# Two PSUM banks of value sums and two of scores in the neighbourhood and windowed attention

## The chip, the cores and the metric

The kernel runs as one program on one core of a Trainium2 chip. The metric is the device time of one execution in microseconds (us). An execution is timed as a whole; the profile adds a span, from the first instruction to the last, and the time of the one execution that was profiled.

## The reference, cut to what matters

Two layers of an encoder over 1024 tokens of width 1024. Each layer projects the normed input once, and four groups of four heads read it: A (latent attention, dense), B (differential attention, dense), C (a window of 128 tokens on each side, with a sink) and D (a neighbourhood of 8 rows by 16 columns on the 64-wide grid, with a bias). The four outputs are joined, projected and added, then an MLP follows. Everything is float32.

```python
def swa_mixer(q, k, v, sinks, cos, sin):          # group C
    ...
    s = jnp.where(valid[None, :, None, None], s, NEG_INF)
    ...
    p = jax.nn.softmax(jnp.concatenate([s, sink], axis=-1), axis=-1)[..., :-1]
    o = jnp.einsum('bnkgqj,bnjkd->bnqkgd', p.astype(v.dtype), vb)

def na_mixer(q, k, v, rpb):                       # group D
    ...
        s = s + jnp.transpose(bias, (0, 2, 1, 3)).astype(jnp.float32)[None]
        p = jax.nn.softmax(s.reshape(B, NA_HEADS, GRID_W, kh * NA_COLS), axis=-1).reshape(s.shape)
        return jnp.einsum('bhwac,bawchd->bwhd', p.astype(v.dtype), v_r)

def reference(...):
    for l in range(DEPTH):
        ...
        mix = jnp.concatenate([rms_norm(y_a, out_g_mla[l]), y_b,
                               rms_norm(y_c, out_g_swa[l]), rms_norm(y_d, out_g_na[l])], axis=-1)
        x = x + mix @ w_out[l]
        h = rms_norm(x, norm2_g[l])
        x = x + jnp.square(jax.nn.relu(h @ w_up[l])) @ w_down[l]
```

## The kernel before

Products are made of two parts, high and low, in three passes (L219 to L221: high by high, high by low, low by high), the parts in the reduced format fp32r. Tokens are reordered for D so that its keys, like those of C, lie in a band: a block of 128 queries sees the key block of its own number and the two beside it.

In a layer the attention runs B, D, C, A, one after the other. `weave` steps through the generator of a group and, after a share of its steps, through a generator of other work, the fill: under B the latent projections and those of D, under D the projections of C and then the upward products of the latent group (`latp`), under C and A the part of the output projection that B's and D's outputs allow (`mix`). Between them it ticks the tails, which are the chains behind a finished head: denominators, their way through DRAM to be spread over the partitions, and norms. A framework orders the instructions of each engine from the dependences and a timeline of its own; on the chip every engine then works through its list in order, and waits on semaphores. SP issues nearly all DMAs, in order too.

The eight PSUM banks of this phase, each a tile of 128 by 512 float32, are split by name for the whole of it: two `mm` (projections and small things), two `tr` (transposes), three `sb` (scores) and one `pv` (value sums).

A head of D or C is `banded`. It has eight key blocks `kb` and makes the scores of query block `i` four blocks ahead: two matmuls into an `sb` bank (L987), an evacuation on VectorE with bias or mask and the running extreme (L1063 in D, L1094 in C), an exponential on ScalarE (L1066, L1097). For a key block, two or three 128x128 pieces are transposed into a `tr` bank (L996), ScalarE writes the high part (`pth`, L193), VectorE the low part (`ptl`, L187; three buffers of each), and `apply` adds the products with the values into `pv` (L1008 with the high part, L1009 with the low one). The 1024 queries fill two banks' worth of sums, so a head has two halves: half 0 takes key blocks 0 to 4, half 1 takes 3 to 7. `zeroed` opens a half with a product with zeros (L1037). `pv_out` takes a finished half out: ScalarE copies the lower 64 partitions (`pvt`, L757) and VectorE adds them to the upper 64 (`y` in D, `yc` in C, L187); `pvt` takes one of the three `ptl` buffers.

B and A are `dense`: scores of 128 queries by 1024 keys in two `sb` banks (L815, evacuated at L817, exponential L820), transposes (L851), value products (L839, L840). Other lines that appear: L266 and L275 are small products of the tails, L647 are transposes of a projection's output, L731 is a product of the latent group's shorter part.

Of the kernel before, what the change touches and what calls it, by code (L numbers as in the profile page):

```python
# [144 lines left out]
class Trunk:  # L145
    def __init__(self, ctx, tc, d, out):
        self.ctx, self.tc, self.nc, self.d, self.out = ctx, tc, tc.nc, d, out
        self.ahead, self.tails = 4, deque()
        pool = lambda **k: ctx.enter_context(tc.tile_pool(**k))
        self.const = pool(name="const", bufs=1)  # L150
        self.xp = pool(name="xp", bufs=8)
        self.big = pool(name="big", bufs=16)
        self.wp = pool(name="wp", bufs=3)
        self.cp = pool(name="cols", bufs=2)
        self.dram = pool(name="dram", bufs=1, space=bass.MemoryType.DRAM)
# [12 lines left out]
    @contextmanager  # L168
    def banks(self, **n):

        self.phase = getattr(self, "phase", 0) + 1
        with self.tc.tile_pool(name=f"ps{self.phase}", bufs=1, space=bass.MemoryType.PSUM,
                               reuse_waits="tile") as self.psum:
            self.nbanks = n
            yield

    def bank(self, tag, shape=(P, 512)):
        return self.psum.tile(list(shape), F, tag=tag, bufs=self.nbanks[tag], name=tag)

    def mm_ps(self):  # L180
        return self.bank("mm")
# [201 lines left out]
    def attention(self, l):  # L383
# [33 lines left out]
        def proj_c():  # L417
            tabs = self.table("64", rb, nc.gpsimd)
            for t in range(2):
                yield from one(T_CQ2[t], xs, self.ev_rope(tabs, qc[:, t]))  # L420
            yield from one(T_CK, xs, self.ev_rope(tabs, kc))
            yield from one(T_CV, xs, self.ev_plain(rb, self.to_values(vc)))
# [2 lines left out]
        y = {"b": [], "d": [], "c": [], "a": []}  # L425
        with ExitStack() as stack, ExitStack() as att:
            self.ap = att.enter_context(sbuf("att"))
            with self.banks(mm=2, tr=2, sb=3, pv=1):
                with sbuf("proj", "right") as self.pp:
                    first = [w_in(t) for t in self.WAVES[0]]  # L430
                    saved = d["x"]
# [32 lines left out]
                               fill, self.RB, self.LB, every=self.EV[0])  # L464
                    self.tails.append(self.mix_b(mix, y["b"], self.gsub[:, l:l + 1]))
                    fill = chain(proj_c(), self.latent_up(l, lat, rows, qa, ka, va))
                    self.weave(self.attn_d(l, qd, kd, vd, y["d"]), fill, self.RD, self.LD, every=self.EV[1])
                gout = lambda n: self.gout[n][:, l]
                self.tails.append(self.mix_group(mix, 2, y["d"], gout("na")))
# [24 lines left out]
                fill = groups_bd()  # L494
                self.weave(self.attn_c(l, qc, kc, vc, y["c"]), fill, self.RC, end=False, every=self.EV[2])
                self.tails.append(self.mix_group(mix, 4, y["c"], gout("swa")))
                self.weave(self.attn_a(l, qa, ka, krd, va, y["a"]), fill, self.RA, self.LA, every=self.EV[3])
                self.tails.append(self.mix_group(mix, 6, y["a"], gout("mla"), nc.vector))
            with self.banks(mm=8):
# [471 lines left out]
    def banded(self, qs, ks, v, y, j, finish, grid=False):  # L971
# [39 lines left out]
        for i in range(self.ahead):  # L1011
            score(i)
        yield True
        pv = self.zeroed()
        held = []
        for kb in range(8):
            if kb + self.ahead < 8:
                score(kb + self.ahead)
            part = parts(kb)
            if kb in (3, 4):  # L1020
                held.append(part)
            if kb <= 4:
                apply(pv, 0, kb, part)
            else:
                apply(pv, 1, kb, part)
            if kb == 4:
                self.pv_out(pv, y, j, 0, grid)
                pv = self.zeroed()
                for i, p in enumerate(held):
                    apply(pv, 1, 3 + i, p)  # L1030
            yield True
        self.pv_out(pv, y, j, 1, grid)

    def zeroed(self):

# [465 lines left out]
```

## Time and profile before

| | us |
|---|---|
| median of 3 runs | 2698.26 (2697.42 to 2702.37) |
| the profiled execution | 2701.14 |
| its span, first to last instruction | 2698.9 |
| busy in the span: TensorE (PE) | 2545.4 (94%) |
| VectorE (DVE) | 1944.6 (72%) |
| ScalarE (ACT) | 1438.1 (53%) |
| GpSimd (POOL) | 1151.6 (43%) |

The span leaves out 2.2 us of the execution's time. PE's share is of matmuls in flight: they are pipelined, and at half clock they count for longer, so 94% is not 94% of what the engine could do. The profile also gives the granted TensorE clock of a stretch, as a share of full speed: 1.00 is 2.4 GHz, 0.50 is 1.2 GHz, and its mean over the program is 0.969. In layer 0 the first score of D is at 323.47 us and the last value product of C at 511.52 us; in layer 1 they are at 1655.09 and 1845.38 us.

### The profile page before, as it was taken

To read this page: it belongs to the slowest core of one execution; us is meant where nothing else is said; L and a number is where in the kernel's file an instruction comes from. 1 tells how busy PE (TensorE), PEld (TensorE's weight loads), DVE (VectorE), ACT (ScalarE), POOL (GpSimd) and SP (SyncE) were. 2 spreads that over 40 slices of the span, in tenths; PEclk is the share of its full clock that TensorE was granted. 3 is DMA by queue.
4 is the path that set the end of the run, shared out by engine and by line. 5 is a ranking of instruction groups with operands and counts; after the bars stand their busy time and mean duration, and the time that the engine had idled before them with its cause. 6 is when DMAs were issued, how large, how long until landed. Compare 5 with 4: busy or idle time off the path is not lost.

```text
span 2698.9 us, 37585 instructions
## 1 busy us (share of the span) xinstructions
PE 2545.4 (94%) x12296; PEld 2109.5 (78%) x12296; DVE 1944.6 (72%) x3368; ACT 1438.1 (53%) x2591; POOL 1151.6 (43%) x816
## 2 busy tenths in 40 slices
PE   8999988999889999999999999789998999999997
PEld 6778876787778887888877788677886788778886
DVE  6777767784966669887568776577749666687776
ACT  4677756663534444444437776566635344444444
POOL 2555633301345554544425655332013455545552
PEclk9989998999999999999999899899999999999998
DMA  5534597421144457444245436963221444664431
GB/s 171 174 94 141 151 268 245 106 89 57 53 140 153 150 166 269 149 139 142 100 128 149 119 114 192 273 199 89 71 71 55 156 150 151 230 219 150 131 102 63
DMA packets 191666, 389.18 MB, mean 144 GB/s; under 512 B 23840, under 2 KB 33008, under 8 KB 191472
## 3 DMA queue, kind: packets, MB, share of 16 engines
q1 hardware_dynamic: 177648, 361.62, 43.3%
q10 hardware_dynamic: 13824, 25.17, 2.7%
q8 instruction: 97, 1.59, 0.2%
q14 instruction: 97, 0.79, 0.1%
HBM read 263.29 MB, written 123.41 MB: 143 GB/s over the span
## 4 chain that ended last, share of the span: by engine, by line
PE 73%; DVE 13%; DMA 5%; ACT 5%; issue 3%; POOL 1%; SPq 0%; DVEq 0%; ACTq 0%; POOLq 0%
PE u L219 8%; PE u L221 8%; PE u L220 8%; PE mm L219 6%; PE mm L220 5%; PE mm L221 5%; PE p L219 5%; PE p L220 5%; PE p L221 5%; PE sb L815 3%; DVE p L817 2%; DVE part L187 2%; PE tr L851 2%; ACT p L820 2%; DVE ptl L187 1%
## 5 line engine op out<-in xcount | busy, mean ns | idle before, releaser
L187 POOL TENSOR_TENSOR wl<-raw,wh 128x512 fp32r<-128x512 f32 x448 | 636.0, 1420 | 699.0 <-ACT wh L193 680.1
L193 ACT ACTIVATE wh<-raw 128x512 fp32r<-128x512 f32 x448 | 281.6, 629 | 575.0 <-PE u L220 314.6
L187 POOL TENSOR_TENSOR wl<-ws,wh 128x512 fp32r<-128x512 f32 (+1 forms) x120 | 151.2, 1262 | 431.2 <-ACT wh L193 427.1
L219 PE MATMUL u<-far,wh 128*128 128x512 f32 x768 | 301.5, 393 | 12.6 <-ACT ev L1247 8.3
L187 DVE TENSOR_TENSOR ptl<-tr,pth 128x512 fp32r<-128x512 f32 (+2 forms) x384 | 239.2, 629 | 88.4 <-ACT pth L193 87.2
L221 PE MATMUL u<-far,wl 128*128 128x512 f32 x768 | 300.8, 392 | 0.8 <-POOL wl L187 0.8
L187 DVE TENSOR_TENSOR raw<-raw 128x512 f32<-128x512 f32 x256 | 222.7, 875 | 107.9 <-POOL wl L187 54.2
L220 PE MATMUL u<-far,wh 128*128 128x512 f32 x768 | 300.5, 391 | 0.0
L193 ACT ACTIVATE pth<-tr 128x512 fp32r<-128x512 f32 (+2 forms) x384 | 206.2, 547 | 123.1 <-PE tr L851 67.2
L820 ACT ACTIVATE p<-p,nm 128x1024 f32<-128x1024 f32 x192 | 220.2, 1147 | 77.3 <-DVE nm L817 72.8
L219 PE MATMUL p<-far,wh 128*128 128x512 f32 x640 | 252.3, 394 | 7.5 <-DVE ev L187 7.5
L221 PE MATMUL p<-far,wl 128*128 128x512 f32 x640 | 251.0, 392 | 1.5 <-POOL wl L187 1.5
L220 PE MATMUL p<-far,wh 128*128 128x512 f32 x640 | 251.2, 392 | 0.0
L815 PE MATMUL sb<-stack 96*128 96x512 f32 x640 | 217.6, 422 | 13.1 <-DVE nm L817 12.8
L187 DVE TENSOR_TENSOR far<-act,far 128x512 fp32r<-128x512 f32 x224 | 210.4, 969 | 14.6 <-ACT far L193 14.6
L187 POOL TENSOR_TENSOR p<-p 128x1024 f32<-128x1024 f32 x64 | 153.5, 2402 | 110.8 <-ACT p L903 103.0
L219 PEld LDWEIGHTS u<-far,wh 128*128 128x128 f32 x768 | 145.4, 189 | 45.2 <-ACT ev L1247 9.2
L851 PE MATMUL tr<-ident,p 128*128 128x128 f32 x1024 | 163.2, 278 | 8.8 <-DVE ptl L187 6.0
L221 PEld LDWEIGHTS u<-far,wl 128*128 128x128 f32 x768 | 145.1, 189 | 32.2 <-POOL wl L187 1.6
L219 PE MATMUL mm<-xh,wh 128*128 128x512 f32 x416 | 168.3, 405 | 1.4 <-DVE part L187 1.2
L220 PEld LDWEIGHTS u<-far,wh 128*128 128x128 f32 x768 | 145.3, 189 | 30.1
L220 PE MATMUL mm<-xl,wh 128*128 128x512 f32 x416 | 165.3, 397 | 0.0
(248 smaller groups left out, 6110.1 us busy)
## 6 DMA issues: line engine op xcount, KB each, us to landing
act<-acts SPq DMA_DIRECT2D x224, 256.0 KB
raw<-in_w_up SPq DMA_DIRECT2D x128, 256.0 KB
acts<-ev SPq DMA_DIRECT2D x128, 256.0 KB
raw<-in_w_down SPq DMA_DIRECT2D x128, 256.0 KB
acts<-ev ACTq DMA_DIRECT2D x96, 256.0 KB
ws<-in_w_in SPq DMA_DIRECT2D x76, 256.0 KB
rz<-drows SPq DMA_DIRECT2D x40, 256.0 KB
stack<-kd SPq DMA_DIRECT2D x32, 256.0 KB
```

The costliest lines, as they stand in the source:

```text
L187: (eng or self.nc.vector).tensor_tensor(out=out, in0=a, in1=b, op=op)
L193: nc.scalar.activation(hi, src, AF.Copy)
L219: mm(ps, w[0], x[0][:, sl], start=start, stop=False)
L220: mm(ps, w[0], x[1][:, sl], start=False, stop=False)
L221: mm(ps, w[1], x[0][:, sl], start=False, stop=stop)
L815: self.nc.tensor.matmul(ps, q[:, qt * P:(qt + 1) * P], k[:, sl], start=i == 0, stop=i == len(passes) - 1)
L817: self.nc.vector.tensor_tensor_reduce(out=p[:, sl], in0=ps, in1=self.zero[:, 0:1].bitcast(F).broadcast_to([P, 512]), scale=-scale, scalar= ...
L820: self.nc.scalar.activation(p, p, AF.Exp, bias=nm[:, 1:2], scale=-1.0, accum_out=z)
L851: nc.tensor.transpose(t[:, k * 256 + i * P:k * 256 + (i + 1) * P], p[:, (j * 2 + k) * P:(j * 2 + k + 1) * P], self.ident)
```

## The change

For D and C the four banks of scores and value sums become two and two. The pool of these banks is closed and opened anew between B and D, and again between C and A, where it is three and one as before. In `banded` each half has its own `pv` bank: half 1 is opened when key block 3 comes, key blocks 3 and 4 are added to both halves at once, and half 0 is taken out after block 4 while half 1 goes on. The list `held` is gone.

```diff
-            with self.banks(mm=2, tr=2, sb=3, pv=1):
+            with self.banks(mm=2, tr=2), ExitStack() as own:
+                def tiles(**n):
+                    own.close()
+                    own.enter_context(self.banks(**n))
+
+                tiles(sb=3, pv=1)
...
                     fill = chain(proj_c(), self.latent_up(l, lat, rows, qa, ka, va))
+                    tiles(sb=2, pv=2)
                     self.weave(self.attn_d(l, qd, kd, vd, y["d"]), fill, self.RD, self.LD, every=self.EV[1])
...
                 self.tails.append(self.mix_group(mix, 4, y["c"], gout("swa")))
+                tiles(sb=3, pv=1)
                 self.weave(self.attn_a(l, qa, ka, krd, va, y["a"]), fill, self.RA, self.LA, every=self.EV[3])
...
-        pv = self.zeroed()
-        held = []
+        pv = [None, None]
         for kb in range(8):
             if kb + self.ahead < 8:
                 score(kb + self.ahead)
             part = parts(kb)
-            if kb in (3, 4):
-                held.append(part)
-            if kb <= 4:
-                apply(pv, 0, kb, part)
-            else:
-                apply(pv, 1, kb, part)
+            for half in range(2):
+                if 3 * half <= kb <= 4 + 3 * half:
+                    if kb == 3 * half:
+                        pv[half] = self.zeroed()
+                    apply(pv[half], half, kb, part)
             if kb == 4:
-                self.pv_out(pv, y, j, 0, grid)
-                pv = self.zeroed()
-                for i, p in enumerate(held):
-                    apply(pv, 1, 3 + i, p)
+                self.pv_out(pv[0], y, j, 0, grid)
             yield True
-        self.pv_out(pv, y, j, 1, grid)
+        self.pv_out(pv[1], y, j, 1, grid)
```

(The rest of the diff lets `bank` look up the pool and the count of a name.) Every engine has as many instructions of each kind as before; only their order and their waits change. In the rows below the changed kernel's lines are some higher: L996 there is the score product L987, L1005 the transposes L996, L1017 and L1018 the value products L1008 and L1009, L1041 the opening L1037, L824 A's score product L815, L221 to L223 the passes L219 to L221, L740 is L731, L277 is L275, L656 is L647, L860 is L851, L268 is L266.

TensorE, layer 0, the middle of D's first head. Before, half 1 is opened and the parts of blocks 3 and 4 are applied once more behind it:

```order
L1008 MATMUL pv<-pth,v 128x256
L731 MATMUL mm<-latp,wh 128x512 x2
L1009 MATMUL pv<-ptl,v 128x256
L996 MATMUL tr<-ident,p 128x128 x3
L266 MATMUL mm<-pairs,rz 128x2 x8
L996 MATMUL tr<-ident,p 128x128 x3
L1037 MATMUL pv<-zero 128x512
L1008 MATMUL pv<-pth,v 128x256
L1009 MATMUL pv<-ptl,v 128x256
L1008 MATMUL pv<-pth,v 128x384
L1009 MATMUL pv<-ptl,v 128x384
L996 MATMUL tr<-ident,p 128x128 x3
```

In the changed kernel, the same engine and layer at D's second head: the opening of a half (here half 0 of that head) and the value products.

```order
L1018 MATMUL pv<-ptl,v 128x384
L1017 MATMUL pv<-pth,v 128x384
L1005 MATMUL tr<-ident,p 128x128 x2
L1041 MATMUL pv<-zero 128x512
L1018 MATMUL pv<-ptl,v 128x384
L996 MATMUL sb<-stack 128x384 x4
L1005 MATMUL tr<-ident,p 128x128 x2
```

The opening stands between the products of the half before it and waits for no evacuation of that half; no products are repeated behind it.

TensorE, layer 0, where D begins. Before, D's scores stand among B's transposes and value products (L851, L839, L840) and the projections (`xh`, `xl`):

```order
L840 MATMUL pv<-ptl,v 128x256
L839 MATMUL pv<-pth,v 128x256
L840 MATMUL pv<-ptl,v 128x256
L987 MATMUL sb<-stack 128x384 x2
L851 MATMUL tr<-ident,p 128x128 x6
L987 MATMUL sb<-stack 128x384 x4
L851 MATMUL tr<-ident,p 128x128 x2
L275 MATMUL mm<-ident,rz 8x128
```

In the changed kernel D's first scores stand behind all of B, at the end of C's last projection, close ahead of the first latent product:

```order
L221 MATMUL mm<-xh_189,wh 128x512
L996 MATMUL sb<-stack 128x256 x2
L996 MATMUL sb<-stack 128x384 x2
L1041 MATMUL pv<-zero 128x512 x2
L222 MATMUL mm<-xl_190,wh 128x512
L223 MATMUL mm<-xh_189,wl 128x512
L221 MATMUL mm<-xh_193,wh 128x512
L222 MATMUL mm<-xl_194,wh 128x512
L223 MATMUL mm<-xh_193,wl 128x512
L996 MATMUL sb<-stack 128x384 x4
L1005 MATMUL tr<-ident,p 128x128 x4
L656 MATMUL mm<-ident,part 128x128 x4
```

The overlap of D's first scores with B is gone from the order, and the projections have moved forward into B's end.

TensorE, layer 0, where C ends. Before, A's scores (L815) stand among the last two heads of C:

```order
L1008 MATMUL pv<-pth,v 128x384
L275 MATMUL mm<-ident,rz 8x128
L987 MATMUL sb<-stack 128x256 x2
L815 MATMUL sb<-stack 128x512 x3
L996 MATMUL tr<-ident,p 128x128 x2
L1009 MATMUL pv<-ptl,v 128x384
L996 MATMUL tr<-ident,p 128x128
L1008 MATMUL pv<-pth,v 128x256
```

In the changed kernel they stand in one block behind C's last value product:

```order
L1005 MATMUL tr<-ident,p 128x128 x2
L1018 MATMUL pv<-ptl,v 128x384
L1017 MATMUL pv<-pth,v 128x384
L1018 MATMUL pv<-ptl,v 128x384
L1017 MATMUL pv<-pth,v 128x256
L1018 MATMUL pv<-ptl,v 128x256
L824 MATMUL sb<-stack 128x512 x18
L860 MATMUL tr<-ident,p 128x128 x2
```

All 42 of A's score products that stood ahead of C's end before stand behind it now, in each layer. From the opening of D's first half to C's last value product, TensorE's list of layer 0 goes from 98 score products of D and C, 168 transposes and 144 products of the fill, with those 42 of A and 4 of A's transposes, to 124, 176 and 125 with none of A's (128 score products counted from D's first score).

## Rows read from the trace of the kernel before

**Rows 1.** The page: busy time by engine, and the granted clock in 40 slices.
```profile
PE 2545.4 (94%) x12296; PEld 2109.5 (78%) x12296; DVE 1944.6 (72%) x3368; ACT 1438.1 (53%) x2591; POOL 1151.6 (43%) x816
...
PEclk9989998999999999999999899899999999999998
```

**Rows 2.** Stretches: busy PE, PEld, DVE, ACT, POOL; granted clock, DMA share, GB/s.
```profile
323.47:357.08 33.61, 33.22 (x188) 28.66 (x186) 20.29 (x52) 20.55 (x48) 17.00 (x13) 1.00 0.87 231
357.08:511.52 154.44, 132.13 (x699) 110.28 (x698) 108.70 (x271) 96.30 (x239) 51.01 (x43) 0.90 0.74 219
511.52:538.52 27.00, 26.17 (x168) 23.13 (x167) 19.78 (x44) 16.66 (x32) 9.66 (x10) 1.00 0.44 118
1686.60:1845.38 158.78, 133.65 (x701) 112.00 (x700) 109.62 (x272) 96.33 (x240) 47.60 (x43) 0.89 0.71 211
```

**Rows 3.** PE's waits, layer 0 (320 to 500 us): total, times, longest.
```profile
PE pv L1008 <- ACT pth L193: 5.6, 5, 2.4
PE pv L1037 <- DVE y L187: 4.6, 2, 3.0
PE mm L220 <- DMA latp<-lat: 3.2, 1, 3.2
PE pv L1037 <- DVE yc L187: 3.0, 1, 3.0
...
PE sb L987 <- DVE nb L1094: 1.2, 4, 0.4
```

**Rows 4.** PE's waits, layer 1 (1690 to 1860 us).
```profile
PE pv L1037 <- DVE y L187: 2.3, 4, 1.4
...
PE pv L1037 <- DVE yc L187: 0.7, 2, 0.3
PE sb L987 <- DVE nb L1063: 0.5, 1, 0.5
```

**Rows 5.** Timeline around two openings, layer 0: start, us, instruction, idle before, releaser.
```profile
414.44 0.80 PE L1037 MATMUL pv<-zero 128*128 128x512 f32 x1 [3.00 <-DVE y L187]
...
413.70 0.68 DVE L187 TENSOR_TENSOR y<-pv,pvt 64x512 f32<-64x512 f32 x1 [2.68 <-DMA yb<-y]
414.42 0.56 DVE L187 TENSOR_TENSOR ptl<-tr,pth 128x384 fp32r<-128x384 f32 x1
...
415.44 0.49 ACT L193 ACTIVATE pth<-tr 128x384 fp32r<-128x384 f32 x1 [3.72 <-PE pv L1008]
...
449.35 1.06 ACT L366 ACTIVATE sq<-y 128x1024 f32<-128x1024 f32 x1 [2.84 <-POOL y L187]
...
449.51 0.20 DVE L768 RECIPROCAL rz<-z 128x8 f32<-128x8 f32 x1 [2.85 <-POOL z L187]
...
450.32 0.80 PE L1037 MATMUL pv<-zero 128*128 128x512 f32 x1 [2.98 <-DVE yc L187]
```

**Rows 6.** Stretches of layer 0 at half clock; two follow the openings of rows 5.
```profile
398.27:401.68 3.41, 3.41 (x11) 3.10 (x12) 3.31 (x12) 2.22 (x8) 0.76 (x1) 0.50 0.98 284
411.92:418.75 6.83, 4.17 (x14) 3.38 (x14) 2.33 (x6) 1.36 (x3) 0.00 (x0) 0.50 1.04 300
449.47:456.29 6.82, 5.57 (x19) 4.95 (x20) 4.47 (x11) 4.21 (x11) 0.69 (x2) 0.50 1.02 330
```

**Rows 7.** A PE gap of 0.92 us, and the ten microseconds behind it.
```profile
427.79 0.38 PE L1008 MATMUL pv<-pth,v 128*128 128x256 f32 x1 [0.92 <-ACT pth L193]
...
427.00:437.00 10.00, 9.21 (x53) 8.02 (x54) 9.73 (x27) 8.48 (x24) 4.38 (x5) 1.00 0.58 202
```

**Rows 8.** The wait for the first latent operand in layer 1.
```profile
1702.92 0.79 PE L220 MATMUL mm<-latp,wh 128*128 128x512 f32 x1 [4.70 <-DMA latp<-lat]
```

**Rows 9.** Chain that ended last: what products cost PE one behind the other.
```profile
480.44 0.70 PE sb L815 x3
...
333.94 0.35 PE sb L987 x2
...
355.68 0.33 PE tr L996 x3
```

More of the change, by code (lines that the diff above doesn't have):

```diff
@@ L147, in __init__ @@
         self.ctx, self.tc, self.nc, self.d, self.out = ctx, tc, tc.nc, d, out
+        self.psum = {}
         self.ahead, self.tails = 4, deque()
@@ L172, in banks @@
         with self.tc.tile_pool(name=f"ps{self.phase}", bufs=1, space=bass.MemoryType.PSUM,
-                               reuse_waits="tile") as self.psum:
-            self.nbanks = n
+                               reuse_waits="tile") as pool:
+            self.psum.update({tag: (pool, bufs) for tag, bufs in n.items()})
             yield
     def bank(self, tag, shape=(P, 512)):
-        return self.psum.tile(list(shape), F, tag=tag, bufs=self.nbanks[tag], name=tag)
+        pool, bufs = self.psum[tag]
+        return pool.tile(list(shape), F, tag=tag, bufs=bufs, name=tag)
     def mm_ps(self):
```

## Prediction

> **What bounds the kernel now.** I read the page first: PE is busy for 94% of the span, VectorE for 72%, ScalarE for 53% [rows 1]. The whole is thus TensorE's, and only what makes TensorE wait, or run at half clock, is to be had. The change touches D and C alone, so next I cut both layers into stretches: the last of B from D's first score to D's first opening, D and C from there to C's last value product, and the first 27 us of A [rows 2]. In the first and the last PE is busy for 33.22 of 33.61 and 26.17 of 27.00 us. In the middle it is busy for 132.13 of 154.44 us in layer 0 and 133.65 of 158.78 in layer 1, at a mean clock of 0.90 and 0.89. So the middle stretches lose 22 and 25 us to waiting, and 0.10 x 154.44 and 0.11 x 158.78, 15 and 17 us, to the clock. No other engine is full there: VectorE has 108.70 of 154.44 us, ScalarE 96.30, the DMA engines a share of 0.74. The stretch runs in lock-step, each engine waiting in turn for the one before.
>
> The list of waits says where PE stands. At the opening of a `pv` bank it waits for VectorE's `y` or `yc`, the end of `pv_out`: 4.6 and 3.0 us in layer 0, 2.3 and 0.7 in layer 1, 10.6 us in all [rows 3, 4]. The other waits are for `pth`, for a latent operand from DRAM and for scores. Two openings make most of it, 3.00 and 2.98 us. The timeline shows what was late there [rows 5]: at the first VectorE stood for 2.68 us until the store of `yb` had left the buffer that `y` writes, at the second for 2.85 us in a reciprocal that waits for GpSimd, and ScalarE for 2.84 in a square that waits for GpSimd. Behind each of the two the clock is at 0.50 for 6.83 us [rows 6]; a gap of 0.92 us has no such stretch behind it [rows 7].
>
> **The change part by part.** No instruction is added or dropped. Four things move.
>
> *The opening no longer waits.* With a bank of its own, half 1 opens at key block 3, when its bank has long been taken out by the head before. All 10.6 us go if nothing else holds PE. But where VectorE or ScalarE is itself stuck behind a DMA or GpSimd, they stay stuck: PE may fill the second `tr` bank and apply what lies ready (a group of three transposes is 0.33 us, a value product as wide as a score product 0.175 [rows 9]), and then waits for `ptl`, which stands in VectorE's list behind the same `y`. I leave 1.0 us at each of the two long ones, and take -8.6; bounds -4.6 (both stay whole) and -10.6.
>
> *The clock.* At half rate 6.83 us do the work of 3.4, so the stretches of rows 6 cost 1.7, 3.4 and 3.4 us. A rest of 1.0 us at an opening is near the gap of rows 7, behind which the clock stayed. I take the first and one of the two long ones, -5.1; bounds 0 and -8.5.
>
> *D begins behind B.* The scores of D's first head no longer stand in B's end; the projections have taken their place, so PE has work there. What comes sooner is the first latent product. Between the middle of C's last projection (its reads release the tiles into which the operand is loaded) and that product PE now has 8 transposes and 7 value products less and two openings more: by rows 9, with the openings at the 0.233 of a product of 512 columns, 8 x 0.11 + 7 x 0.175 - 2 x 0.233 = 1.6 us. It already waits 3.2 and 4.7 us there [rows 3, 8], so it waits 1.6 longer in each layer: +3.2; bounds 0 (fewer of D's loads stand ahead of it in the queue of SP) and +3.2.
>
> *A begins behind C, and scores have two banks.* At C's end nothing stands between the last transposes and the last value products, which need 0.49 us of ScalarE and 0.56 of VectorE [rows 5]: +1.0 in each layer, +2.0, bounds 0 and +4. With two `sb` banks a score waits for the evacuation two before it, not three. Those waits are 1.2 and 0.5 us now [rows 3, 4]; I let them double, +1.7; bounds 0 and +6, which is the two stuck places of rows 5 felt once more at a score.
>
> The sum is -8.6 - 5.1 + 3.2 + 2.0 + 1.7 = -6.8 us. Against the profiled execution's 2701.14 that is 2694.3; against the median of the runs, which lies 2.9 lower, 2698.26 - 6.8 = 2691.5, a fall of 0.25%. About 0.2%, 5.4 us, is what a measurement of this kernel can tell from no change, so this is just beyond it.
>
> A second account checks that moving work between stretches is by itself neutral. From the order, layer 0's middle loses 42 score products of A and 19 of the fill at 0.233 us and 4 transposes of B's kind, and gains 30 of D's scores at 0.175 and 8 transposes at 0.11 [rows 9]: -14.2 - 0.4 + 5.3 + 0.9 = -8.4 us. B's end changes by 4.4 - 5.3 - 0.9 = -1.8, and A's beginning by +9.8 + 0.4 = +10.2. The three add up to nothing. So the middle has to shrink from 154.44 to 146.0 us for no change at all, and by my terms it comes to about 139 (layer 0 has 5.6 of the 8.6 us, all of the 5.1, and half of the costs).
>
> **The rivals.** *Nothing to measure.* The stuck engines hold PE all the same: the openings give only the 4.6 us that were not long stalls, the clock nothing, and 6.9 us of costs stand against it: +2.3, 2700.6; with the latent wait at its lower bound -0.9, 2697. For it: both long stalls have their cause outside the sums [rows 5]. Against it: ScalarE stood for 3.72 us for want of value products that waited behind the opening, which shows the lock-step at work.
> The Trainium skill, TensorE: Matmul & The Clock Gate, section HAM oscillation — how this bites in real kernels, tells of a kernel in which double-buffering PSUM gave no further gain; by that result the first two terms would be nothing and the sum +6.9, 2705. The trace's 10.6 us at the openings speaks against taking it over whole.
>
> *Slower: D and C lose their cover.* Before, 42 score products of A stand within C; after, they stand behind it. If the middle is set by the chain of VectorE and ScalarE, with its 108.70 us of VectorE in 154.44, and not by PE's share of work, it stays at 154.4 us, and PE's 8.4 us come on top in each layer: +16.8, 2715; with half of that, +8.4, 2707. It decides at 146.0 us for layer 0's middle: above that the layer is slower. For it: VectorE keeps nearly all its work in the middle while PE gives 8.4 us away. Against it: VectorE is busy for only 0.70 of the middle, and in the ten microseconds of rows 7 it did 9.73 of 10.00.
> The Trainium skill, Perfetto Trace Analysis, section Optimization Strategy, says that where the most contended engine changes over time, interleaving the regimes may help. The change does the reverse at both ends of D and C, and by that rule alone this rival would hold, at its +16.8. The trace agrees that the ends with overlap are the fuller ones (33.22 of 33.61 us).
>
> *That the change does nothing it says* the order excludes: the second opening stands at key block 3, with no product repeated behind it.
>
> **How the numbers follow.** I give the forecast, faster, 0.42; no measurable change 0.34; slower 0.24. The time is the forecast's, 2691.5. Its own range is 2676 to 2696: at the low end every term is at its better bound (-10.6 - 8.5 and no costs, -19, 2679) with a little for waits on `pth` (5.6 us in layer 0) that may go as well. The whole range reaches into the slower rival to some of its full price: 2676 to 2711.
>
> **What would show it.** Right: no waits at the opening (L1041 after) for `y` or `yc`; layer 0's middle, from the first opening to the last value product, well under 146 us; no half-clock stretch of 6.8 us behind the places where the third head of D and the first of C turn to half 1; the wait for the latent operand at about 4.8 and 6.3 us; waits of scores below 4 us in all. Wrong: waits for `ptl` or `pth` that grow by what the openings lose (then the first rival), or a middle above 146 us with PE waiting for scores or value products, and VectorE no busier (then the second). If the gain is much above 10 us, the lock-step cost more than PE's waits at the openings show.

## The result, and the profile after

The changed kernel takes 2719.59 us, median of 4 runs (2713.05 to 2725.22), against 2700.32 for the kernel before on the same chip (2697.42 to 2705.94): ratio 1.0064, 95% interval 1.0039 to 1.0089. In a second set (e4) it is 2717.88 us, ratio 1.0058 (1.0042 to 1.0075). It is 16 to 19 us slower; forecast was a gain of 6.8, in a range up to 2711. The profiled execution took 2713.05 us, its span is 2711.3.

The page of the changed kernel answers to [rows 1]: busy time by engine, and the granted clock in 40 slices.

```profile
PE 2559.2 (94%) x12296; PEld 2114.6 (78%) x12296; DVE 1942.2 (72%) x3368; ACT 1438.2 (53%) x2591; POOL 1148.6 (42%) x816
...
PEclk9989989999999999999999899899999999999998
```

The same number of instructions, and a TensorE that is busy 13.8 us longer, while the other engines are not. The page says no more, so next come the stretches, columns as in [rows 2]. In each layer they are D and C from the first opening to the last value product, from there to A's first value product, and on to A's 120th; in layer 0 also the rest of A.

```profile
358.40:503.10 144.70, 125.88 (x663) 103.69 (x661) 104.67 (x271) 95.36 (x251) 45.31 (x42) 0.91 0.80 236
503.10:521.20 18.10, 16.65 (x69) 13.22 (x70) 10.38 (x26) 8.58 (x16) 4.32 (x6) 0.81 0.09 30
521.20:582.60 61.40, 58.71 (x361) 50.79 (x359) 49.48 (x106) 40.84 (x72) 8.83 (x7) 0.97 0.34 93
582.60:636.60 54.00, 50.18 (x331) 42.64 (x329) 41.42 (x90) 36.22 (x62) 0.00 (x0) 1.00 0.16 55
...
1697.80:1841.60 143.80, 124.16 (x663) 101.27 (x661) 105.05 (x271) 95.62 (x252) 45.70 (x42) 0.92 0.81 238
1841.60:1860.50 18.90, 16.56 (x61) 13.39 (x62) 9.45 (x22) 8.06 (x14) 3.69 (x5) 0.73 0.10 29
```

And the kernel before, from C's last value product to A's first, in both layers:

```profile
511.50:514.20 2.70, 1.88 (x13) 1.44 (x11) 1.43 (x5) 2.62 (x6) 0.00 (x0) 1.00 0.40 114
...
1845.40:1848.10 2.70, 1.88 (x14) 1.46 (x12) 1.44 (x3) 2.63 (x6) 0.01 (x1) 1.00 0.47 138
```

The middle did shrink, from 154.44 and 158.78 us to 144.70 and 143.80. But 2.70 us between C and A have become 18.10 and 18.90, at a clock of 0.81 and 0.73. Before, A was 42 score products deep by C's end; now it starts from nothing, and its first value product comes 15.4 and 16.2 us later. By the prediction's count of moved work (its second account, for layer 0) that should have been 10.2.

TensorE's waits in D and C: first layer 0, to be held against [rows 3] (the opening is L1041 now, the score L996, the value product L1017).

```profile
PE sb L996 <- DVE nb L1067: 3.6, 3, 3.1
PE pv L1017 <- ACT pth L195: 3.4, 2, 2.0
...
PE mm L222 <- DMA latp<-lat: 1.8, 1, 1.8
PE sb L996 <- DVE nb L1098: 1.5, 1, 1.5
...
PE pv L1041 <- DVE yc L189: 0.9, 2, 0.7
PE mm L221 <- DMA latp<-lat: 0.8, 1, 0.8
```

And layer 1, against [rows 4, 8]:

```profile
PE pv L1017 <- ACT pth L195: 5.8, 5, 2.3
...
PE sb L996 <- DVE nb L1098: 2.3, 4, 1.1
PE mm L222 <- DMA latp<-lat: 2.1, 1, 2.1
PE sb L996 <- DVE nb L1067: 1.6, 2, 0.9
...
PE mm L221 <- DMA latp<-lat: 1.0, 1, 1.0
...
PE pv L1041 <- DVE y L189: 0.3, 1, 0.3
PE mm L740 <- DMA latp<-lat: 0.2, 1, 0.2
```

The openings wait 0.9 and 0.3 us, 1.2 in place of 10.6. Scores wait 3.6 + 1.5 + 2.3 + 1.6 = 9.0 us in place of 1.7. The latent operand is waited for less, not more: 1.8 + 0.8 = 2.6 us in layer 0 and 2.1 + 1.0 + 0.2 = 3.3 in layer 1, in place of 3.2 and 4.7.

The start of A in layer 0, from the chain that ended last:

```profile
503.10 0.40 PE pv L1018
503.53 0.60 ACT pvt L766
504.15 0.70 DVE yc L189
...
504.92 2.39 POOL yc L189
507.33 1.06 ACT sq L368
508.39 1.14 ACT p L829 x2
509.57 0.44 PE tr L860 x2
510.01 3.09 PE mm L268 x16
```

C's last product, its copy out of the bank, GpSimd's part of `yc`, and then on ScalarE the squares of `yc` ahead of A's first two exponentials: only at 509.57 is there a block of A to transpose, 6.5 us after C's last product. The other 11.6 us up to A's first value product are TensorE's own list: sixteen small products of a tail (L268), more of A's scores and transposes, and products of the output projection. The timeline of TensorE there (`sb<-stack` are A's score products), and two stretches by the clock, one in each layer:

```profile
503.33 4.87 PE L824 MATMUL sb<-stack 96*128 96x512 f32 x18
509.57 0.44 PE L860 MATMUL tr<-ident,p 128*128 128x128 f32 x2 [1.38 <-ACT p L829]
...
521.16 0.28 PE L848 MATMUL pv<-pth,v 128*128 128x256 f32 x1
...
510.00:516.90 6.90, 6.90 (x26) 6.08 (x25) 3.12 (x10) 2.90 (x6) 0.81 (x4) 0.51 0.00 0
1848.00:1858.30 10.30, 10.07 (x36) 8.90 (x37) 4.17 (x13) 3.85 (x9) 0.00 (x0) 0.50 0.01 2
```

TensorE issues 18 score products in a row, stands for 1.38 us, and from 510.0 on runs at half clock, 1.2 GHz, for 6.9 us; in layer 1 a stretch of 10.3 us begins in the same place. The kernel before has no half clock there: its first 27 us of A ran at 1.00 [rows 2].

### The profile page after: what moved, and what is told of

The parts are those of the page before. It is cut to its first block, busy times and chain, and to the rows that moved or that the text cites. A ratio compares the mean times of both kernels' runs of the same rounds, so it can differ in the third digit from the quotient of the medians.

```text
span 2711.3 us, 37601 instructions
## 1 busy us (share of the span) xinstructions
PE 2559.2 (94%) x12296; PEld 2114.6 (78%) x12296; DVE 1942.2 (72%) x3368; ACT 1438.2 (53%) x2591; POOL 1148.6 (42%) x816
## 4 chain that ended last, share of the span: by engine, by line
PE 71%; DVE 13%; DMA 6%; ACT 5%; issue 4%; POOL 1%; SPq 1%; DVEq 0%; ACTq 0%; POOLq 0%
PE u L221 8%; PE u L223 8%; PE u L222 8%; PE mm L221 6%; PE mm L222 5%; PE mm L223 5%; PE p L221 5%; PE p L222 5%; PE p L223 5%; PE sb L824 3%; DVE p L826 2%; PE tr L860 2%; DVE part L189 2%; ACT p L829 2%; DVE ptl L189 2%
## 5 line engine op out<-in xcount | busy, mean ns | idle before, releaser
L221 PE MATMUL u<-far,wh 128*128 128x512 f32 x768 | 301.7, 393 | 9.2 <-ACT ev L1251 5.9
L223 PE MATMUL u<-far,wl 128*128 128x512 f32 x768 | 300.9, 392 | 2.6 <-POOL wl L189 2.6
L221 PE MATMUL p<-far,wh 128*128 128x512 f32 x640 | 251.3, 393 | 8.1 <-DVE ev L189 8.1
L223 PE MATMUL p<-far,wl 128*128 128x512 f32 x640 | 250.8, 392 | 1.2 <-POOL wl L189 1.2
L824 PE MATMUL sb<-stack 96*128 96x512 f32 x640 | 221.9, 430 | 12.9 <-DVE nm L826 12.4
L221 PEld LDWEIGHTS u<-far,wh 128*128 128x128 f32 x768 | 145.3, 189 | 41.9 <-ACT ev L1251 7.2
L860 PE MATMUL tr<-ident,p 128*128 128x128 f32 x1024 | 166.0, 281 | 11.7 <-DVE ptl L189 7.5
L223 PEld LDWEIGHTS u<-far,wl 128*128 128x128 f32 x768 | 145.3, 189 | 34.0 <-POOL wl L189 3.5
L221 PE MATMUL mm<-xh,wh 128*128 128x512 f32 x416 | 168.2, 404 | 3.3 <-DVE part L189 3.2
L222 PEld LDWEIGHTS u<-far,wh 128*128 128x128 f32 x768 | 145.4, 189 | 30.6 <-DVE far L189 0.5
L826 DVE CUSTOM_DVE_ANT_0 p<-sb,zero,nm 128x512 f32<-128x512 f32 x192 | 142.6, 744 | 35.3 <-PE sb L824 30.6
```

What stands on the lines that cost most here:

```text
L221: mm(ps, w[0], x[0][:, sl], start=start, stop=False)
L222: mm(ps, w[0], x[1][:, sl], start=False, stop=False)
L223: mm(ps, w[1], x[0][:, sl], start=False, stop=stop)
L824: self.nc.tensor.matmul(ps, q[:, qt * P:(qt + 1) * P], k[:, sl], start=i == 0, stop=i == len(passes) - 1)
L826: self.nc.vector.tensor_tensor_reduce(out=p[:, sl], in0=ps, in1=self.zero[:, 0:1].bitcast(F).broadcast_to([P, 512]), scale=-scale, scalar= ...
L860: nc.tensor.transpose(t[:, k * 256 + i * P:k * 256 + (i + 1) * P], p[:, (j * 2 + k) * P:(j * 2 + k + 1) * P], self.ident)
```

## The experiments

Three things come with the change: other banks in D and C, another order of products in D and C, and pools that are closed and opened again between B and D and between C and A. To have banks without re-opening, some kernels keep one pool with a bank "flex" that is lent by name:

```python
if tag in ("sb", "pv"):
    sets = {"sb": ("sb0", "sb1"), "pv": ("pv0",)}[tag] + (("flex",) if self.shared == tag else ())
    self.turn[tag] += 1
    slot, n = sets[self.turn[tag] % len(sets)], 1
```

Banks are given as scores/values. "Early" is the changed order of products (the second group of sums opens at key block 3), "held" the older one. Medians are of 4 to 12 runs, ratios against the kernel before in the same set (2699.05 to 2702.84 us).

| run | B | D, C | A | order | re-opened | us | ratio (95%) |
|---|---|---|---|---|---|---|---|
| before | 3/1 | 3/1 | 3/1 | held | - | 2700 | 1 |
| after (e4) | 3/1 | 2/2 | 3/1 | early | B-D, C-A | 2717.88 | 1.0058 (1.0042, 1.0075) |
| e1 | 3/1 | 3/1 | 3/1 | held | B-D, C-A | 2735.01 | 1.0128 (1.0112, 1.0144) |
| e2 | 3/1 | 2/2 | 3/1 | early | - | 2710.07 | 1.0036 (1.0023, 1.0049) |
| e3 | 2/2 | 2/2 | 2/2 | early | - | 2713.15 | 1.0050 (1.0036, 1.0065) |
| e5 | 3/1 | 2/2 | 2/2 | early | B-D | 2692.18 | 0.9965 (0.9949, 0.9981) |
| e6 | 2/2 | 2/2 | 3/1 | early | C-A | 2738.15 | 1.0129 (1.0109, 1.0148) |
| e8 | 3/1 | 3/2, one `tr` | 3/1 | early | - | 2792.14 | 1.0326 (1.0305, 1.0347) |
| e9 | 3/1 | 2/1 | 3/1 | held | - | 2707.40 | 1.0018 (1.0004, 1.0031) |
| e10 | 3/1 | 2/2 | 2/2 | early | B-D, C-A | 2696.36 | 0.9986 (0.9977, 0.9996) |
| e11 | 3/1 | 2/2 | 2/2 | early | - | 2686.54 | 0.9960 (0.9948, 0.9973) |
| e12 | 3/1 | 2/2 | 2/2 | held | B-D | 2695.28 | 0.9990 (0.9980, 0.9999) |
| e13 | 2/2 | 2/2 | 2/2 | early | B-D | 2742.03 | 1.0164 (1.0144, 1.0183) |
| e14 | 3/1 | 3/1 | 2/2 | held | - | 2699.39 | 0.9999 (0.9989, 1.0010) |
| e15 | 3/1 | 2/2 | 2/1 | early | - | 2684.38 | 0.9945 (0.9931, 0.9960) |
| e16 | 3/1 | 2/2 | 2/1, then 3/1 | early | - | 2691.67 | 0.9970 (0.9959, 0.9982) |
| e17 | 3/1 | 2/2 | 2/2 | held | - | 2693.77 | 0.9983 (0.9973, 0.9993) |
| e18 | 3/1 | 2/2 | 2/1 | early | B-D, C-A | 2703.60 | 1.0007 (0.9994, 1.0020) |
| e19 | 3/1 | 3/1 | 3/1 | held | C-A | 2717.27 | 1.0064 (1.0050, 1.0077) |

Theory 1: the re-opening is the loss, since the order shows every instruction on the new banks behind the last one on the old. Theory 2: the third score bank of D and C is. The first four runs:

**e1_reopened**: the kernel before, its pool re-opened at both places.

```diff
+                    tiles(sb=3, pv=1)
                     self.weave(self.attn_d(...
+                tiles(sb=3, pv=1)
                 self.weave(self.attn_a(...
```

> The kernel before, with the pool of score and value banks closed and opened anew at both places, but with three and one banks throughout and the held parts as before. Theory 1 (the re-opening puts D behind B and A behind C, and that is the loss): about 2716 to 2722, as slow as the changed kernel or a little slower; from C's last value product to A's 120th value product about 79 us where the kernel before has 64.0 and 63.9, with a half-clock stretch in it; openings still wait for the evacuation, some 8 to 11 us. Theory 2 (two score banks are the loss, through 9 us of waits of scores where there were about 2): within 4 us of the kernel before, 2697 to 2704.

**e2_shared**: the new banks and order, lent by name, nothing re-opened.

```diff
-            with self.banks(mm=2, tr=2, sb=3, pv=1):
+            with self.banks(mm=2, tr=2, sb0=1, sb1=1, flex=1, pv0=1):
...
+                    self.shared = "pv"
                     self.weave(self.attn_d(...
...
+                self.shared = "sb"
                 self.weave(self.attn_a(...
```

> The changed banded with two and two banks in D and C, but no pool is closed: one bank of the pool is lent, as third score bank in B and A and as second value bank in D and C. Theory 1: D's scores overlap B again and A's overlap C, the openings do not wait, so faster than the kernel before by the gain of the middle beyond what moved, 1.3 and 6.1 us, and with the loss at the seams gone: 2688 to 2697. Theory 2: scores wait as in the changed kernel, 7 us more than before, and it stays at 2710 or more.

**e3_whole**: two and two for the whole phase, which also shares the first projections' banks out anew.

```diff
-            with self.banks(mm=2, tr=2, sb=3, pv=1):
+            with self.banks(mm=2, tr=2, sb=2, pv=2):
...
-                        return [(self.bank(a), self.bank(b)) for a, b in (("sb", "sb"), ("sb", "tr"), ("tr", "pv"))]
+                        return [(self.bank(a), self.bank(b)) for a, b in (("sb", "sb"), ("tr", "tr"), ("pv", "pv"))]
```

> Two score and two value banks for the whole phase of attention, B and A too, nothing re-opened. Theory 1: the seams overlap, so no loss there; B and A have one score bank less, each score tile of which needs two banks, so PE waits for VectorE more in B and A: the waits of L815 were 36.0 us with weight loads counted, and a tenth to a half more of these is 4 to 18 us; 2695 to 2712. Theory 2: slower than the changed kernel, above 2720, as scores lack a bank everywhere.

**e4_again**: the changed kernel once more, in the same set.

> The changed kernel once more, for a second profile. Both theories: 2713 to 2725; from C's last value product to A's 120th about 79.5 us in both layers, of which some 5 are the clock, and the middles near 144.7 and 143.9 us. If the half-clock stretch at A's beginning is absent in this profile and the time is the same, the clock there was chance and not the loss.

Re-opening alone costs 34 us, more than the whole change, so theory 1 holds; but without it the change still loses 0.36%, so it isn't all. The next four separate the two seams and the banks.

**e5_seam_bd**: the changed kernel without the second re-opening; A stays on two and two.

```diff
-                tiles(sb=3, pv=1)
                 self.weave(self.attn_a(...
```

> The changed kernel with one re-opening left: three score banks and one value bank are traded for two and two between B and D, and A then stays on two and two, so nothing is re-opened between C and A. Theory 1 (the seam at A's start is the costly one: the middle is at its break-even in the changed kernel, A's beginning some 5 us a layer over it): A loses its seam, 2706 to 2713 us, and A's gap before its first key loads (2.2 us in layer 1) is gone. Theory 2 (the seam between B and D is the costly one): no gain at A, and A pays for its third score bank, 2716 to 2724 us.

**e6_seam_ca**: the other seam alone, B on two and two.

```diff
-                tiles(sb=3, pv=1)
+                tiles(sb=2, pv=2)
                 with sbuf("proj", "right") as self.pp:
...
-                    tiles(sb=2, pv=2)
                     self.weave(self.attn_d(...
```

> The changed kernel with the other re-opening left: B, D and C run on two score banks and two value banks, and three and one come back between C and A alone (the first projections take their bank pairs from scores, transposes and values in order). Theory 1 (the seam at A's start is the costly one): 2716 to 2722 us, with the gap before A's first key loads and the half clock behind it as in the changed kernel. Theory 2 (the seam between B and D is the costly one): 2704 to 2713 us, with B's end back at 84 to 86 us.

**e8_tr_lent**: three score banks kept; the second value bank of D and C is a transpose bank, lent.

```diff
-            with self.banks(mm=2, tr=2, sb=3, pv=1):
+            with self.banks(mm=2, sb=3, tr0=1, flex=1, pv0=1):
```

> Two value banks in D and C and three score banks throughout, nothing re-opened: the second value bank is one of the two banks of the 128-wide transposes, lent by name in D and C. Theory 2 (the third score bank given up is what e2 lost; the openings are a gain of 8 to 10 us): the openings' waits are gone, score waits stay at 2 us a layer, transposes in D and C wait some us more with one bank: 2692 to 2700 us. Rival (the early openings don't gain, since what moves ahead of them is paid elsewhere, or one transpose bank costs as much as one score bank): 2703 to 2715 us.

**e9_two_scores**: the kernel before, with the third score bank idle in D and C.

```diff
+                    self.shared = None
                     self.weave(self.attn_d(...
...
+                self.shared = "sb"
                 self.weave(self.attn_a(...
```

> The kernel before, its held transposed parts and one value bank as they were, with two score banks in D and C: the third lies idle there, nothing is re-opened. Theory 2 (the lost score bank is the price): 2711 to 2722 us, with score waits in the middle of 7 to 10 us a layer in place of 2. Theory 1 (score banks cost little): 2699 to 2705 us.

e5 is faster than the kernel before, and 0.93% (25 us) faster than the changed kernel: the loss sits at A's start. e6 misses both expectations; e13 below shows why. e8 is the dearest miss: with one transpose bank, TensorE waits for `pth` in layer 0's middle:

```profile
PE pv L1016 <- ACT pth L199: 20.8, 28, 4.6
```

28 waits, 20.8 us in place of 5.6 [rows 3]. e9 puts the third score bank at 0.18% (0.04 to 0.31), some 5 us, under what theory 2 expected. But e5 differs from the changed kernel by A's banks too. Four runs for that:

**e10_seam_ca_22**: e5 with the seam at A put back, same banks on both sides.

```diff
+                tiles(sb=2, pv=2)
                 self.weave(self.attn_a(...
```

> The kernel of e5 with the re-opening between C and A put back, but with the same banks on both sides of it (two of scores, two of values), so that only the seam differs. If the seam is the loss (A's scores can't stand among C's any more and D and C lose them as cover): 2710 to 2720 us, with A's beginning back at 78 to 80 us a layer. If A's banks are what separates e5 from the changed kernel (two value banks serve A better than three score banks): 2690 to 2698 us.

**e11_lent_to_a**: e2 with the lent bank left to the values in A.

```diff
-                self.shared = "sb"
                 self.weave(self.attn_a(...
```

> The kernel of e2 with the lent bank kept as a value bank through A: banks as in e5 in every stage, but nothing is re-opened between B and D either. If the seam between B and D is itself a gain (it keeps D's scores out of B's end): near e2, 2703 to 2711 us. If e2 was slower than e5 for A's banks: 2688 to 2697 us, as e5.

**e12_held**: e5 with the held order of before in D and C.

```diff
-            for half in range(2):
-                if 3 * half <= kb <= 4 + 3 * half:
...
+            if kb in (3, 4):
+                held.append(part)
```

> The kernel of e5 with D's and C's older order of products: one group of value sums open at a time, the transposed parts of the two shared blocks held and applied at the second opening; banks and the one seam as in e5. If the openings gain because the second group opens early, beside work: 2698 to 2706 us, with waits for value copies at the openings between 0 (the second bank) and 10 us a layer (as before). If the second bank alone frees the opening, whatever the order: 2689 to 2696 us and no such waits.

**e13_b_two**: e5 with B on two and two.

```diff
-                tiles(sb=3, pv=1)
+                tiles(sb=2, pv=2)
                 with sbuf("proj", "right") as self.pp:
```

> The kernel of e5 with two score and two value banks in B as well (first projections over bank pairs in order), the re-opening between B and D kept, with the same banks on both sides. Against e3, which differs from it by that re-opening alone, and against e5, which differs by B's banks alone. If B's third score bank is what e3 lost: 2708 to 2716 us, with B up to its 100th score at 217 us a layer in place of 184 to 189. If the seam between B and D is the gain: 2690 to 2697 us.

e10 surprised: the same two seams as the changed kernel, and some 20 us less; e11 is some 20 us less than e2. So A's banks matter, with a seam or without. e13 is some 50 us over e5: B needs its third score bank (from its first score product to its hundredth it takes 215.4 and 213.8 us in e13, 187.5 and 182.8 in e5; e3 is some 25 us over e11, nothing re-opened in either), and so e6 was slow from B on. e12 lies 0.25% over e5. The last six runs (the first four in one set) ask what it is about A's banks.

**e14_a_two**: the kernel before, with the third score bank lent to the values in A alone.

```diff
+                self.shared = "pv"
                 self.weave(self.attn_a(...
```

> The kernel before with one edit: the third score bank is lent to the value sums in A alone, so A runs on two and two; D and C keep three score banks, one value bank and the held parts; nothing is re-opened. If A gains by its second value bank itself (with two value banks its stretch behind the 120th product took 52.1 us a layer in place of 54.0, its beginning behind the seam 76.8 in place of 79.4, so some 9 us): 2688 to 2695 us. If what costs is a bank that changes its use between C and A, whatever A runs on: 2702 us or more, with fewer than 39 of A's scores ahead of C's last product.

**e15_a_two_one**: e11 with the lent bank idle in A.

```diff
+                self.shared = None
                 self.weave(self.attn_a(...
```

> The kernel of e11 with A on two score banks and one value bank, the lent bank idle there: no bank changes its use between C and A, and A lacks the second value bank as well as the third score bank. If A's second value bank is what separates e11 from e2: 2695 to 2704 us or more, A's stretch behind its 120th product at 54 us or more. If the change of use between C and A is: 2686 to 2692 us.

**e16_late_third**: e2, the lent bank idle until A's fifth tile of queries, then a score bank.

```diff
             def probs(qt):
+                if h == 0 and qt == 4:
+                    self.shared = "sb"
```

> The kernel of e2 (A on three score banks and one value bank, nothing re-opened) with the lent bank idle for A's first four tiles of queries and a score bank from the fifth: A's first scores then don't wait for the bank that C's last value sums hold. If e2 lost A's lead over C's end (18 and 9 of A's scores stand ahead of C's last product there, 39 in e11): 2690 to 2700 us and a lead of some 39 again. If A's banks are all of it: 2705 to 2712 us.

**e17_lent_held**: e11 with the held order.

```diff
-                    if kb == 3 * half:
-                        pv[half] = self.zeroed()
...
+            if kb in (3, 4):
+                held.append(part)
```

> The kernel of e11 with D's and C's older order (one group of value sums open at a time, two transposed parts held), all else alike. If the early second opening is worth what the re-opened pair says (e12 less e5: 3 us): 2687 to 2693 us. If the openings' waits come back whole (some 8 to 10 us of TensorE's waits a layer in the kernel before) in spite of the second value bank: 2696 to 2704 us.

**e18_seams_two_one**: the changed kernel with A on two and one.

```diff
-                tiles(sb=3, pv=1)
+                tiles(sb=2, pv=1)
                 self.weave(self.attn_a(...
```

> The changed kernel with both re-openings, A on two score banks and one value bank in place of three and one. If the third score bank, which is taken out of C's value banks, is what separates the changed kernel from e10: 2690 to 2700 us, as e10 on two and two, and A's stretch behind its 120th product at 52 us in place of 54.0. If A's second value bank separated them: 2712 to 2722 us.

**e19_seam_ca_old**: the kernel before, re-opened between C and A alone.

```diff
+                tiles(sb=3, pv=1)
                 self.weave(self.attn_a(...
```

> The kernel before with the pool of score and value banks re-opened between C and A alone, three and one on both sides: A's 42 scores that stand ahead of C's last product go behind it, nothing else changes. The prediction's term for this was 2.0 us (0 to 4), its slower rival 8.4 to 16.8: 2700 to 2705 us if the term was right, 2708 to 2717 us if the rival was, and 2718 us or more if most of the 34 us of e1 is this seam's.

e15 has the fewest banks in A and is the fastest of all, 0.55% (some 15 us) below the kernel before, though its interval overlaps e11's; e14 trades A's third score bank for a second value bank and gains nothing. So A, where it keeps its lead, doesn't need a second value bank. What e2 lost goes with a bank that changes from values to scores between C and A: in e16, with A on three and one as in e2 but the third bank handed over four tiles later, A's lead is back and the time is 18 us less. Not all of it need be the lead: behind the seams, where A has none, the third score bank still costs 14 us (the changed kernel against e18). The timeline of e2 at C's end, A's score products alone, and then that of e15 (C's last product is at 503.07 and 502.41):

```profile
502.30 0.93 PE L823 MATMUL sb<-stack 96*128 96x512 f32 x3
504.09 0.97 PE L823 MATMUL sb<-stack 96*128 96x512 f32 x3 [0.73 <-DVE nm L825]
```

```profile
493.08 0.96 PE L824 MATMUL sb<-stack 96*128 96x512 f32 x3
494.56 0.91 PE L824 MATMUL sb<-stack 96*128 96x512 f32 x3
495.82 0.91 PE L824 MATMUL sb<-stack 96*128 96x512 f32 x3
496.80 0.86 PE L824 MATMUL sb<-stack 96*128 96x512 f32 x3
...
499.93 0.86 PE L824 MATMUL sb<-stack 96*128 96x512 f32 x3
501.61 0.96 PE L824 MATMUL sb<-stack 96*128 96x512 f32 x3
```

In e15 A's scores are threaded through C's last transposes and value products; in e2 none stands between 494.7 and 502.3. Counted in the traces, A has this many score products out ahead of C's last value product (layer 0, layer 1): before 42, 42; e5, e11, e14, e15 and e16 39, 39; e2 18, 9; the changed kernel, e10, e18 and e19 none. A bank handed over the other way, from scores to values in e14, costs little of the lead.

## Why the prediction was wrong, by its own steps

One path through the table takes the change apart along the prediction's terms: before to e9, the third score bank of D and C given up, +0.18%; e9 to e11, the second value bank and the early opening (and A on two and two), -0.58%; e11 to e5, the seam between B and D, +0.05%; e5 to the changed kernel, the seam between C and A with A back on three and one, +0.93%. In the sum that is the +0.58% of e4, 16 us.

**The step that failed is "A begins behind C", +2.0, bounds 0 and +4.** On that path it costs 25 us. e19 makes this one move alone, in the kernel before: +0.64% (0.50 to 0.77), 17 us. The prediction looked only at C's own tail (what stands between the last transposes and the last products) and asked 1.0 us for it. It didn't ask what A's first value product waits for when A starts from nothing. The stretches of e19, layer 0's and layer 1's middle and the first part of A:

```profile
354.90:505.00 150.10, 126.24 (x652) 106.64 (x651) 101.92 (x247) 89.87 (x228) 49.20 (x43) 0.86 0.76 222
505.00:520.90 15.90, 14.39 (x67) 10.99 (x67) 9.83 (x24) 8.41 (x15) 4.47 (x6) 0.89 0.11 36
...
1700.70:1848.30 147.60, 119.37 (x652) 100.11 (x652) 100.83 (x247) 89.75 (x228) 47.74 (x43) 0.93 0.76 226
1848.30:1861.70 13.40, 13.08 (x67) 10.31 (x66) 10.14 (x26) 8.20 (x15) 3.43 (x5) 0.97 0.15 41
```

A's first value product comes 15.9 and 13.4 us after C's end in place of 2.70, and the middle, rid of A's scores, gives back 4.3 and 11.2 us. The two moved stretches account for some 9 us more in layer 0 and nothing in layer 1; B's first 100 scores of layer 1, where nothing was moved, took 182.6 us in the trace of before and 188.2 in that of e19, so single profiles can't place the 17 us more closely.

The late first value product is not the price by itself. In e10 A starts from nothing too, its first value product 16.0 and 19.4 us after C's end, at a clock of 0.79 and 0.82:

```profile
503.30:519.30 16.00, 14.03 (x57) 10.91 (x57) 7.53 (x19) 7.36 (x13) 3.31 (x6) 0.79 0.11 34
...
1836.90:1856.30 19.40, 17.40 (x71) 13.50 (x72) 11.11 (x26) 8.98 (x17) 5.16 (x7) 0.82 0.17 57
```

Yet with A on two and two on both sides of the seam this costs 0.21%, 6 us (e5 to e10). D's and C's middle, rid of A's scores, gives 8.6 and 2.9 us back there (145.3 and 145.4 us, 153.9 and 148.3 in e5); the two profiled runs lie further apart than the medians, so they don't place the rest. The other 19 us of the 25 come with A's banks behind the seam. Even the 6 lie above the prediction's bound.

**So the second account's "moving work is by itself neutral" failed, and the slower rival was right in the number, not in the mechanism.** The rival that D and C lose their cover was priced at 8.4 to 16.8 us; e19 measures 17, the changed kernel 16 to 19. But it had the middle stay at 154.4, and said that only above 146.0 the layer is slower. In the changed kernel's trace layer 0's middle fell to 144.70 (the prediction's own terms make it about 139), and the loss came at A's beginning, which paid 15.4 us in place of the neutral 10.2. The two together are 5.7 us longer in layer 0 and 1.2 in layer 1, of the 12 us between the two profiled executions. That the rival's price came out is luck.
The Trainium skill, Perfetto Trace Analysis, section Optimization Strategy, says that interleaving regimes in which different engines are the most contended may help, which spoke for this rival. The runs agree in sign: undoing one such interleaving cost 17 us in e19 and 6 in e10.

**The openings, -8.6, and their clock, -5.1.** The waits went as said, 10.6 to 1.2 us. As a gain in time they were right too, where A's start is left alone: e9 to e11 (one value bank and held order to two and early; A's banks, which differ as well, are worth nothing by e14) is 1.0018 to 0.9960, 0.58% or 16 us, against 13.7 predicted. The order alone is 0.23 to 0.25% of it (e17 to e11, e12 to e5), 6 to 7 us; the bank alone is the rest, 0.35% (e9 to e17), some 9 us. The profiles don't show the gain wait by wait: TensorE's waits for `pth` in D and C are 8.6 and 5.5 us in e11, where D opens earlier and the stretches are longer, and 1.4 and 3.3 in e9. The first rival, that nothing is left to measure, is out.
The Trainium skill, TensorE: Matmul & The Clock Gate, section HAM oscillation — how this bites in real kernels, reports a kernel in which double-buffered PSUM gave no further gain. These runs show a gain.
The clock term was counted too high from the start: in the two long stretches of [rows 6] PE was busy for only 4.17 and 5.57 of the 6.83 us, so half rate cost it 2.1 and 2.8 us there, not 3.4 each, and the rest is the wait that the first term already has. It did not hold in the changed kernel either. The middles have less at half rate, 27.3 and 23.9 us in place of 30.7 and 34.1, but A's start has 6.9 and 10.3 us of it, which cost half of that.

**Two score banks, +1.7, bounds 0 and +6.** e9 measures 0.18%, 5 us, within the bounds: a term mis-sized. In the changed kernel scores wait 9.0 us, above the 4 named as the limit. **D begins behind B, +3.2.** The latent operand was waited for less, so the term has the wrong sign there; the seam as a whole costs 0.05 to 0.07% where D goes on with two value banks (e5 against e11, e12 against e17), 1 to 2 us, the intervals overlapping. But it costs 17 us in e1 against e19, with three and one on both sides, and some 30 in e13 against e3, with two and two on both sides. Why it is dear there and cheap where the banks change is left open.

**What is left of the changed kernel.** e11 shows what the banks and the order are worth without the seams, -11 us; the changed kernel is 27 us above it. The two seams with A on two and two are 7 of those (e10), giving up A's second value bank behind them 6 (e18), taking the third score bank 14. e18, at 2703.60 us, lies between its two expectations: both banks count behind the seams, though without seams A misses neither (e15). For the third score bank, e10, which has only two, shows part in A itself:

```profile
519.30:580.10 60.80, 58.80 (x370) 51.20 (x368) 51.51 (x115) 41.79 (x74) 10.31 (x7) 1.00 0.36 94
580.10:632.20 52.10, 49.14 (x332) 43.53 (x331) 41.84 (x89) 35.98 (x62) 0.00 (x0) 1.00 0.17 57
```

A's rest is 52.1 us where the changed kernel takes 54.00; from C's end to A's last product it is 128.9 against 133.5, and e18, on two and one, has some 129 too. That is some 4.5 us a layer, 9 of the 14. Where the remaining 5 go, and the 6 of the second value bank, isn't shown. The clock does not settle it: its mean is 0.972 over e10's twelve runs and 0.969 over e4's six, but the runs of either at 0.970 take 2694.98 to 2697.05 and 2715.86 to 2720.14 us, some 20 apart. e14, too, has a rest of A 1.9 us shorter in each layer and no gain in the whole; why is open.

## What to carry to other kernels

A move of work between two stages is not neutral where stage two has run ahead into the tail of stage one. Look at the latency from stage two's first product to its first consumer (here 13 to 19 us a layer), hold it against what stage one gives back, and expect the price to depend on the banks of stage two (6 us in e10, 17 in e19, 25 in the changed kernel); the prediction, which took moved work to be neutral, had 2. Closing and opening a PSUM pool at a stage's border, or handing over a bank that the tail of one stage and the head of the next both want, takes that lead away; leave such a bank idle until the new stage is under way (e16), or do without it (e15). The version to keep is e15: the second value bank and the early opening in D and C, nothing re-opened, A on two score banks and one value bank, 2684.38 us, 0.55% below the kernel before (e11, with A on two and two, can't be told from it).

## What was not expected of the hardware

The third score bank is no help in the rest of A, behind the 120th value product: with it the rest takes 54.00 us (in the kernel before, the changed kernel and e19 alike), and 52.0 with two score banks and one value bank in e15.

```profile
567.00:619.00 52.00, 48.59 (x333) 43.45 (x331) 41.77 (x89) 35.29 (x62) 0.00 (x0) 1.00 0.16 57
```

TensorE is busy for 48.59 us there, 50.18 in the changed kernel, for nearly the same work (333 and 331 instructions, 66 and 63 of them score products). The records differ in the order of the list, score products put singly between others in e15; that this is the cause was not tried. And the runs of one kernel spread as widely as the effects here: e5's go from 2682.68 us at a mean granted clock of 0.974 to 2703.13 at 0.969, with one of 2693.45 at 0.968, so the clock accounts for part of the spread at most. With twelve runs the intervals are still 0.10 to 0.16% to either side.
